# Low parts of four late weight matrices of layer 2, made in layer 1's MLP and read back from memory

## The chip, the cores and the metric

One core of one Trainium2 chip runs the whole program in one launch. The metric is the device time of one execution in microseconds; lower is better. PE is the matmul engine, DVE, ACT and POOL (GpSimd) are the vector, scalar and general engines, SP only issues transfers here.

## The reference

Two layers of a decoder trunk for 256 tokens of width 1024, all in float32. Of one layer (shortened):

```python
h = rms_norm(x, norm_mix[l]); z = h @ w_in[l]
...
o_all = jnp.stack([o_a, o_b, o_c], axis=2).reshape(B, T, N_MIXERS, MIX_WIDTH)
y = jnp.einsum('btnc,ncd->btnd', o_all, w_branch[l])
g = jax.nn.sigmoid(gm.reshape(B, T, N_MIXERS, D_MODEL))
x = x + jnp.sum(g * y, axis=2) @ w_out[l]
h2 = rms_norm(x, norm_mlp[l])
x = x + jnp.square(jax.nn.relu(h2 @ w_up[l])) @ w_down[l]
```

The mixers are A (sparse attention over the top keys of an indexer), B (sliding window with sinks) and C (compressed, selected and window branches).

## The kernel before

**Products in three parts.** Every weight is read once, as float32, and multiplied on PE in float32r. For float32 accuracy each 128 x 512 piece of a weight matrix is split (`wsplit`, L208): ACT copies it to float32r, the high part `wh` (L214), and DVE subtracts that from the raw piece, the low part `wl` (L215). `mm3` (L218) then makes three matmuls, activation high by `wh`, high by `wl`, low by `wh` (L219 to L221), for each of the two halves of 128 tokens, so six per piece. `raw` has 5 buffers of 128 x 1024 (two pieces), `wh` and `wl` 4 each.

```python
with tc.high_priority(offset=LEAD):
    wh = til(wsp, [P, 512], F32R, "wh")
    wl = til(wsp, [P, 512], F32R, "wl")
    act.copy(wh[:, :n], raw2d)
    dve.tensor_tensor(out=wl[:, :n], in0=raw2d, in1=wh[:, :n].bitcast(F32), op=ALU.subtract)
```

**The order of a layer.** `PLAN` lists the projections in the order in which `linear` (L223) streams them: queries, keys and values, the indexer, then the merge gates (gB1 is the gate of mixer B, columns 512 to 1023) and the branch projections (bB1 likewise). The last nine entries are gB1, gA1, gC1, bB1, bB0, bC0, gA0, bC1. Beside each piece a share of the attention of A, B or C is emitted, by the rate that stands next to the name; A's follows last. Then w_out and the MLP: `up` (L1041) makes 512 hidden columns from 8 pieces of w_up, `down` multiplies them by w_down, in the order up(0), up(1), down(0), up(2) and so on to up(7), down(6), down(7). In `up` each weight piece is the stationary side (L1052, L1053), and PE's results are squared and split by ACT and DVE (L1059 to L1065).

**What sets the order of instructions.** The code emits the work; a scheduler of the framework, with a simulated time line, then fixes the order on each engine, and the weight splits go 600 places ahead of where they are emitted (`LEAD`). At run time every engine works in that order and waits on semaphores. All loads of weights are issued by SP (L206, L243), in order. POOL has only a few multiplies for rotary (L356) and powers for the norms (L320, L465, L476).

**Between layer 1's w_out and its MLP** the new residual x (L1034) is transposed on PE, and each of the 16 blocks of 128 x 128 is scaled into `hT`: ACT makes its high part (L275), then DVE its low part (L276).

**Layer 2's late stage.** On the clock of the trace gA1 and gC1 run from about 606 to 630, bB1 and bB0 to about 649, then the attention of mixer C ends (L569 and L570 scores, L576 and L580 maximum, L587 exponential, L617 transposes, L200 and L201 their split, L646 a sum, L867 the compressed branch, L881 the selected branch), with pieces of bC0 between.

Of the kernel before, what the change touches and what calls it, by code (L numbers as in the profile page):

```python
# [8 lines left out]
F32 = mybir.dt.float32  # L9
F32R = mybir.dt.float32r  # L10
BF16 = mybir.dt.bfloat16
AF = mybir.ActivationFunctionType
ALU = mybir.AluOpType
# [3 lines left out]
P = 128  # L17
T = 256
NT = 2
D = 1024  # L20
# [3 lines left out]
DEPTH = 2  # L24
# [7 lines left out]
)  # L32
ACT_SET = "exp_and_others"
LEAD = 600
WARM = 9
SPLIT = 'A'
BUFS = dict(wraw=5, wsp=4, zp=3, mp=3, t4p=3, hlp=2, khp=2, pp=2, ptp=2, st=2, sm=3, gmp=3)

O_QA, O_KA, O_VA, O_IQ, O_IK, O_IW = 0, 512, 640, 768, 1024, 1088
O_QB, O_KB, O_VB = 1092, 1604, 1732  # L40
O_QC, O_KC, O_VC, O_KS, O_VS, O_KW, O_VW = 1860, 2372, 2500, 2628, 2756, 2884, 3012
O_GC, O_GM = 3140, 3164
# [50 lines left out]
def trunk(ctx: ExitStack, tc: tile.TileContext, A: dict, out: bass.AP):  # L93
    nc = tc.nc
    pe, dve, act, pool, sp = nc.tensor, nc.vector, nc.scalar, nc.gpsimd, nc.sync

    def mk(name, bufs=1, space=None):
        kw = {} if space is None else {"space": space}
        return ctx.enter_context(tc.tile_pool(name=name, bufs=bufs, **kw))
# [3 lines left out]
    wraw, wsp = mk("wraw", BUFS["wraw"]), mk("wsp", BUFS["wsp"])  # L103
    zp, mp, t4p = mk("zp", BUFS["zp"]), mk("mp", BUFS["mp"]), mk("t4p", BUFS["t4p"])
    hlp, khp = mk("hlp", BUFS["hlp"]), mk("khp", BUFS["khp"])
    qtp, vtp = mk("qtp", 2), mk("vtp")
    gmp, pp, ptp, otp = mk("gmp", BUFS["gmp"]), mk("pp", BUFS["pp"]), mk("ptp", BUFS["ptp"]), mk("otp", 2)
    fin = mk("fin", 2)
    st, sm = mk("st", BUFS["st"]), mk("sm", BUFS["sm"])
    ps_lin = mk("ps_lin", 4, PSUM)  # L110
    ps_s = mk("ps_s", 2, PSUM)
# [5 lines left out]
    def til(pool_, shape, dt, tag):  # L117
        uid[0] += 1
        return pool_.tile(shape, dt, tag=tag, name=f"{tag}_{uid[0]}")
# [13 lines left out]
    pieces = []  # L133
# [9 lines left out]
    with tc.high_priority(offset=0):  # L143
        act.dma_start(out=gcols, in_=A["gcols"])
        act.preload_act_table_set(ACT_SET)
        first_load(0, 1)
# [56 lines left out]
    def wload(src, kk, n):  # L203
        raw = til(wraw, [P, 1024], F32, "raw")
        v = raw[:, :kk * n].rearrange("p (k n) -> p k n", k=kk)
        sp.dma_start(out=v, in_=src)  # L206
        return v

    def wsplit(raw2d):
# [10 lines left out]
        pe.matmul(ps, lhsT=ah, rhs=bl, start=False, stop=False)  # L220
        pe.matmul(ps, lhsT=al, rhs=bh, start=False, stop=last)  # L221

    def linear(ps, xh, xl, w, c0, n, more=None):  # L223

        kc = w.shape[0] // P
        narrow = n <= 256
        kk, per = (4, 2) if narrow else (2, 1)
        c1, n1 = more or (0, 0)  # L230
        at_k = 0
        while at_k < kc:
            if pieces:
                raw = pieces.pop(0)
                kk = raw.shape[1]
            else:
                rows = slice(at_k * P, (at_k + kk) * P)
                raw = til(wraw, [P, 1024], F32, "raw")[:, :kk * (n + n1)].rearrange("p (k n) -> p k n", k=kk)
                early = ahead.pop() if ahead else 0
                for at, col, width in ((0, c0, n), (n, c1, n1)):  # L240
                    if width:
                        with tc.high_priority(offset=early):
                            sp.dma_start(out=raw[:, :, at:at + width], in_=w[rows, col:col + width].rearrange("(k p) n -> p k n", p=P))  # L243
            parts = []
            for j in range(0, kk, per):
                wh, wl = wsplit(raw[:, j:j + per, :].rearrange("p k n -> p (k n)"))
                for i in range(per):
                    cs = slice(i * (n + n1), (i + 1) * (n + n1))
                    parts.append((wh[:, cs], wl[:, cs]))
            steps = [(j, t) for j in range(kk) for t in range(NT)]  # L250
            if at_k + kk == kc:
                steps = [(j, t) for t in range(NT) for j in range(kk)]
            for j, t in steps:
                k, tk = at_k + j, slice(t * P, (t + 1) * P)
                mm3(ps[t][:, :n + n1], xh[:, k, tk], xl[:, k, tk], *parts[j], k == 0, k == kc - 1)
            at_k += kk
            yield kk * (n + n1) / 1024
# [33 lines left out]
    xh, xl = x_pair()  # L291
# [11 lines left out]
    for l in range(DEPTH):  # L303
        w_in = A["w_in"][l]
# [137 lines left out]
        def queries(m, c0, i):  # L442
            m.qT = til(qtp, [P, 8, T], F32R, "qT")
            m.rq = [til(lay, [P, 8], F32, f"rq{i}{t}") for t in range(NT)]
            ps = two_banks()
            yield from linear(ps, xh, xl, w_in, c0, 512)
            posts.append(queries_post(m, i, ps))

        def queries_post(m, i, ps):
# [254 lines left out]
        def branch_keys_1(m):  # L704
            m.kT = til(vtp, [P, 2, 2, 2, T], F32R, "kTC")
            m.v = [new_v(f"C{b}", F32R) for b in range(2)]
            ps = two_banks()
            yield from linear(ps, xh, xl, w_in, O_KC, 512)
            posts.append(branch_keys_1_post(m, ps))

        def branch_keys_1_post(m, ps):
# [183 lines left out]

        def gate_half(n, hf, dst, spare=None):
            ps = two_banks()
            yield from linear(ps, xh, xl, w_in, O_GM + n * D + hf * 512, 512)
            if n == 1:
                sg = pair[:, hf]  # L900
                dst[hf] = sg
            else:
                sg = til(vtp, [P, NT, 512], F32, spare) if spare else til(gmp, [P, NT, 512], F32, "sg")
                dst[hf] = sg
            for t in range(NT):
                act.activation(sg[:, t, :], ps[t], AF.Tanh, scale=hrstd[t])
# [3 lines left out]
        def branch_half(n, hf, m, sg):  # L910
            first = hf not in begun
            begun.add(hf)
            ps = two_banks()
            cs = slice(hf * 512, (hf + 1) * 512)
            yield from linear(ps, m.o[0], m.o[1], A["w_branch"][l][n], hf * 512, 512)
            for t in range(NT):
                y = merged[t][:, cs] if first else til(mp, [P, 512], F32, "m")
                dve.scalar_tensor_tensor(out=y, in0=sg[hf][:, t, :], scalar=1.0, in1=ps[t], op0=ALU.add, op1=ALU.mult)  # L918
                if not first:
                    dve.tensor_tensor(out=merged[t][:, cs], in0=merged[t][:, cs], in1=y, op=ALU.add)  # L920
# [35 lines left out]
        for hf in range(2):  # L956
            for key, n, m, sg in (("A", 0, MA, sgA), ("B", 1, MB, sgB), ("C", 2, C, sgC)):
                name = f"g{key}{hf}"
# [70 lines left out]
        for hf in range(2):  # L1029
            cs = slice(hf * 512, (hf + 1) * 512)  # L1030
            ps = two_banks()
# [8 lines left out]
        def up(gi):  # L1040
            L, S, X, O = (ps_lin, "lin"), (ps_s, "s"), (ps_t, "t"), (ps_o, "o")  # L1041
            ph = [bank(*b) for b in ((L, L, X, O) if gi == 0 else (S, S, L, L) if gi == 1 else (S, S, X, O))]
            src = A["w_up"][l][:, gi * 512:(gi + 1) * 512].rearrange("(a k p) n -> a p k n", p=P, k=2)
            for a in range(KC // 2):
                raw = wload(src[a], 2, 512)
                for j in range(2):
                    wh, wl = wsplit(raw[:, j, :])
                    k = 2 * a + j
                    for f in range(4):

                        fs = slice(f * P, (f + 1) * P)
                        pe.matmul(ph[f], lhsT=wh[:, fs], rhs=both_h[:, k].rearrange("p i t -> p (i t)"), start=k == 0, stop=False)  # L1052
                        pe.matmul(ph[f][:, :T], lhsT=wl[:, fs], rhs=hh[:, k, :], start=False, stop=k == KC - 1)  # L1053
            ah, al = new_o()
            for b in range(2):
                r = til(mp, [P, 512], F32, "m")
                for i in range(2):
                    part = r[:, i * T:(i + 1) * T]
                    act.copy(part, ph[2 * b + i][:, T:])  # L1059
                    dve.tensor_tensor(out=part, in0=ph[2 * b + i][:, :T], in1=part, op=ALU.add)  # L1060
                s = til(zp, [P, 512], F32, "z")
                dve.scalar_tensor_tensor(out=s, in0=r, scalar=0.0, in1=r, op0=ALU.max, op1=ALU.mult)
                s3 = s.rearrange("p (f q) -> p f q", f=2)
                act.copy(ah[:, 2 * b:2 * b + 2, :], s3)
                dve.tensor_tensor(out=al[:, 2 * b:2 * b + 2, :], in0=s3, in1=ah[:, 2 * b:2 * b + 2, :].bitcast(F32), op=ALU.subtract)  # L1065
            return ah, al

        def down(gi, a_):
# [9 lines left out]
            for f, hf in order:  # L1078
# [13 lines left out]
                elif f == 3:  # L1092
# [3 lines left out]
                                products(f_, hf, t)  # L1096
                    yield hf

        prev = up(0)
        for gi in range(1, NG):  # L1100
            nxt = up(gi)
            if gi == 1:
                acc = [[bank(ps_lin, "lin") for _ in range(NT)] for _ in range(2)]
            run(down(gi - 1, prev))
            prev = nxt
        r2 = []
        for t in range(NT):
            ss = sum_sq(t)
# [4 lines left out]
        if l + 1 < DEPTH:  # L1113
            xh, xl = x_pair()
# [39 lines left out]
```

## Time and profile before

| | us |
|---|---|
| median of 3 runs (916.27 to 917.17) | 916.95 |
| the profiled execution | 918.04 |
| its span | 916.3 |
| PE busy | 898.1 (98%) |
| DVE busy | 728.8 (80%) |
| ACT busy | 611.5 (67%) |
| POOL busy | 76.3 (8%) |
| layer 1's MLP, about | 281 to 467 |
| gA1, gC1, bB1, bB0 of layer 2, about | 606 to 649 |

A busy PE is only the sum of its instructions' stretches. What changes the time is where PE has nothing to do, so the table is a start and the stretches of PE's idle time are the thing to find: windows tell in which stage, the waits tell behind whom, and the timelines tell whether that engine was late or only its releaser.

### The profile page before, as it was taken

How to read it: one execution, taken by the hardware profiler on the slowest of the kernel's cores; microseconds unless marked ns; L12 is line 12 of the kernel's file. 1: busy time of each engine (PE TensorE's matmuls, PEld its weight loads, DVE VectorE, ACT ScalarE, POOL GpSimd, SP SyncE). 2: the span in 40 equal slices, each digit the busy share in tenths (PEclk: the TensorE clock that was granted, in tenths of full speed). 3: DMA queues.
4: the chain of work that ended last, by engine and by line, in shares of the span. 5: the costliest groups of instructions: out<-in, count | busy, mean ns of one | idle time of the engine just before them, and what ended most of it. 6: DMA issues, size and time to landing. Idle time of an engine off the chain costs nothing.

```text
span 916.3 us, 14300 instructions
## 1 busy us (share of the span) xinstructions
PE 898.1 (98%) x4785; PEld 749.6 (82%) x4785; DVE 728.8 (80%) x1558; ACT 611.5 (67%) x1369; POOL 76.3 (8%) x68
## 2 busy tenths in 40 slices
PE   8999999999999999999999999999899999999998
PEld 5888888877778888888879878878787788888886
DVE  5899989789986766666789999977998776666665
ACT  6787888767656655555578778877686575555553
POOL 0533011000000000000014420300000000000000
PEclk9999999999999999999999999999999999999999
DMA  8745556531455666666646555555134556666652
GB/s 301 211 141 168 161 162 184 161 115 60 128 174 167 199 192 193 194 185 188 193 137 187 165 157 170 177 181 151 61 93 137 182 162 208 185 187 196 191 184 92
DMA packets 84426, 153.15 MB, mean 167 GB/s; under 512 B 9600, under 2 KB 26880, under 8 KB 84352
## 3 DMA queue, kind: packets, MB, share of 16 engines
q1 hardware_dynamic: 84208, 152.22, 55.0%
q8 instruction: 37, 0.61, 0.3%
q14 instruction: 37, 0.30, 0.1%
q10 hardware_dynamic: 144, 0.02, 0.0%
HBM read 151.17 MB, written 1.05 MB: 166 GB/s over the span
## 4 chain that ended last, share of the span: by engine, by line
PE 84%; DVE 8%; issue 3%; DMA 2%; ACT 1%; POOL 1%; SPq 0%; DVEq 0%; ACTq 0%
PE lin L220 17%; PE lin L219 17%; PE lin L221 17%; PE s L1052 6%; PE s L1053 3%; DVE wl L215 3%; PE t L1052 3%; PE o L1052 3%; PE s L569 2%; DMA raw<-in_w_in 2%; PE lin L1052 2%; PE o L694 2%; PE t L1053 1%; PE o L1053 1%; PE t L617 1%
## 5 line engine op out<-in xcount | busy, mean ns | idle before, releaser
L215 DVE TENSOR_TENSOR wl<-raw,wh 128x512 fp32r<-128x512 f32 (+1 forms) x568 | 388.2, 693 | 139.2 <-ACT wh L214 134.6
L214 ACT CAST wh<-raw 128x512 fp32r<-128x512 f32 (+1 forms) x568 | 346.1, 619 | 209.2 <-PE lin L221 103.6
L220 PE MATMUL lin<-wl,xTh 128*128 128x512 f32 (+2 forms) x512 | 194.8, 384 | 3.7 <-DVE wl L215 3.2
L221 PE MATMUL lin<-wh,xTl 128*128 128x512 f32 (+2 forms) x512 | 187.0, 370 | 0.0
L219 PE MATMUL lin<-wh,xTh 128*128 128x512 f32 (+2 forms) x512 | 167.3, 379 | 1.6 <-ACT wh L214 1.6
L220 PE MATMUL lin<-wl,oTh 128*128 128x512 f32 x352 | 137.8, 392 | 0.0
L221 PE MATMUL lin<-wh,oTl 128*128 128x512 f32 x352 | 137.1, 391 | 0.0
L220 PEld LDWEIGHTS lin<-wl,xTh 128*128 128x128 f32 x512 | 96.2, 188 | 24.6 <-DVE wl L215 9.8
L219 PE MATMUL lin<-wh,oTh 128*128 128x512 f32 x352 | 113.5, 393 | 0.0
L219 PEld LDWEIGHTS lin<-wh,xTh 128*128 128x128 f32 x512 | 93.9, 189 | 19.0 <-ACT wh L214 3.6
L221 PEld LDWEIGHTS lin<-wh,xTl 128*128 128x128 f32 x512 | 96.0, 188 | 14.3 <-issue 0.2
L221 PEld LDWEIGHTS lin<-wh,oTl 128*128 128x128 f32 x352 | 66.1, 188 | 13.9 <-issue 0.2
L220 PEld LDWEIGHTS lin<-wl,oTh 128*128 128x128 f32 x352 | 66.1, 188 | 13.4 <-DVE hT L918 0.2
L1052 PE MATMUL s<-hT,wh 128*128 128x512 f32 x224 | 76.2, 395 | 0.0
L219 PEld LDWEIGHTS lin<-wh,oTh 128*128 128x128 f32 x352 | 65.2, 188 | 12.9
L587 ACT ACTIVATE pr<-s,mx,rq 128x256 f32<-128x256 f32 (+1 forms) x128 | 64.6, 517 | 1.3 <-DVE mx L580 1.3
L1053 PE MATMUL s<-hT,wl 128*128 128x256 f32 x224 | 52.7, 280 | 0.0
L1053 PEld LDWEIGHTS s<-hT,wl 128*128 128x128 f32 x224 | 42.1, 188 | 5.6
L1052 PE MATMUL t<-hT,wh 128*128 128x512 f32 x112 | 44.5, 397 | 0.0
L1052 PE MATMUL o<-hT,wh 128*128 128x512 f32 x112 | 44.0, 393 | 0.0
L1052 PEld LDWEIGHTS s<-hT,wh 128*128 128x128 f32 x224 | 38.6, 188 | 5.1
L200 ACT CAST pt<-t 128x512 fp32r<-128x512 f32 x36 | 21.2, 588 | 22.0 <-PE t L617 21.7
(202 smaller groups left out, 1328.8 us busy)
## 6 DMA issues: line engine op xcount, KB each, us to landing
raw<-in_w_in SPq DMA_DIRECT2D x91, 512.0 KB, 3.8
raw<-in_w_up SPq DMA_DIRECT2D x64, 512.0 KB, 3.8
raw<-in_w_down SPq DMA_DIRECT2D x64, 512.0 KB, 4.1
raw<-in_w_branch SPq DMA_DIRECT2D x24, 512.0 KB, 3.8
raw<-in_w_out SPq DMA_DIRECT2D x16, 512.0 KB, 3.8
raw<-in_w_ck SPq DMA_DIRECT2D x8, 512.0 KB, 3.9
raw<-in_w_cv SPq DMA_DIRECT2D x8, 512.0 KB, 4.2
raw<-in_w_in SPq DMA_DIRECT2D x8, 324.0 KB, 3.6
```

The costliest lines, as they stand in the source:

```text
L200: act.copy(hi, src)
L214: act.copy(wh[:, :n], raw2d)
L215: dve.tensor_tensor(out=wl[:, :n], in0=raw2d, in1=wh[:, :n].bitcast(F32), op=ALU.subtract)
L219: pe.matmul(ps, lhsT=ah, rhs=bh, start=first, stop=False)
L220: pe.matmul(ps, lhsT=ah, rhs=bl, start=False, stop=False)
L221: pe.matmul(ps, lhsT=al, rhs=bh, start=False, stop=last)
L569: pe.matmul(ps3[:, i * per:(i + 1) * per, :], lhsT=q[:, h, t * P:(t + 1) * P], rhs=rhs(j, h // 4), start=(i == 0 and j == 0), stop=False)
L587: act.activation(p3[:, r, :], ps3[:, r, :], AF.Exp, bias=mx[:, r:r + 1], scale=rq[r // per], accum_out=den[:, r:r + 1])
L617: pe.transpose(ps[:, i * P:(i + 1) * P], pr[:, i * P:(i + 1) * P], ident)
L694: pe.matmul(dst, lhsT=lhs_v(m.v, kt, g), rhs=p4[:, :, kt, :], start=i == 0 and kt == 0, stop=i == len(parts) - 1 and kt == t)
L1052: pe.matmul(ph[f], lhsT=wh[:, fs], rhs=both_h[:, k].rearrange("p i t -> p (i t)"), start=k == 0, stop=False)
L1053: pe.matmul(ph[f][:, :T], lhsT=wl[:, fs], rhs=hh[:, k, :], start=False, stop=k == KC - 1)
```

## The change

Four matrices of layer 2 are named in `STORED`: gA1, gC1 (8 pieces each), bB0, bB1 (4 each), 24 pieces. During layer 1's MLP a generator, `split_ahead`, makes one piece with each raw load of w_up from up(1) to up(6): SP loads the 256 KB piece (`pr`), ACT copies the high part (`pt`), DVE subtracts (`ptl`), SP stores the low part to memory. In layer 2, `linear` loads each raw piece of these matrices alone (256 KB in place of 512 KB for two), ACT makes `wh` as before, and a DMA that POOL issues brings the low part: odd pieces into the four `wl` buffers, even ones into two new buffers, `low`. `KEPT` is empty, so its branches don't run. All line numbers after the new code move: L215 is now L220, L219 to L221 are L224 to L226, L275 and L276 are L340 and L341, L867 and L881 are L932 and L946.

```diff
+KEPT = ()
+STORED = ('gA1', 'gC1', 'bB0', 'bB1')
...
+    lowp = mk("lowp", 2)
+    low_parts = mk("low_parts", 1, bass.MemoryType.DRAM)
...
-        sp.dma_start(out=v, in_=src)
+        last_load[:] = [sp.dma_start(out=v, in_=src).ins]
...
+    def split_ahead():
+
+        room = rooms()
+        for name in KEPT + STORED:
+            w, c0 = columns(1, name)
+            for k in range(w.shape[0] // P):
+                raw = til(pp, [P, 512], F32, "pr")
+                with tc.issue_after(last_load[0]):
+                    sp.dma_start(out=raw, in_=w[k * P:(k + 1) * P, c0:c0 + 512])
+                if name in KEPT:
+                    to = next(room)
+                    wh, wl = to[:, 0:512], to[:, 512:1024]
+                    kept.append((wh, wl))
+                else:
+                    wh, wl = til(ptp, [P, 512], F32R, "pt"), til(ptp, [P, 512], F32R, "ptl")
+                act.copy(wh, raw)
+                dve.tensor_tensor(out=wl, in0=raw, in1=wh.bitcast(F32), op=ALU.subtract)
+                if name in STORED:
+                    mem = til(low_parts, [P, 512], F32R, f"lo{name}{k}")
+                    sp.dma_start(out=mem.bitcast(F32), in_=wl.bitcast(F32))
+                    stored[name, k] = mem
+                yield
...
+            parts = []
+            if (name, at_k) in stored:
+                kk = 1
+                raw = til(wraw, [P, 1024], F32, "raw")
+                sp.dma_start(out=raw[:, 0:512], in_=w[at_k * P:(at_k + 1) * P, c0:c0 + 512])
+                wl = til(wsp, [P, 512], F32R, "wl") if at_k % 2 else til(lowp, [P, 512], F32R, "low")
+                pool.dma_start(out=wl, in_=stored[name, at_k])
+                with tc.high_priority(offset=LEAD):
+                    wh = til(wsp, [P, 512], F32R, "wh")
+                    act.copy(wh, raw[:, 0:512])
+                parts.append((wh, wl))
...
-            for j in range(0, kk, per):
+            for j in range(0, 0 if parts else kk, per):
...
                 raw = wload(src[a], 2, 512)
+                if gi:
+                    next(aside, None)
...
+        aside = split_ahead() if l + 1 < DEPTH else iter(())
...
+        for _ in aside:
+            pass
```

(`issue_after` places the load of `pr` behind the last raw load on SP.)

PE in the late stage, before, where the selected branch of mixer C begins (`lin_8025` is bC0, `o` the results of attention, `s` its scores, `t` its transposes):

```order
L219 MATMUL lin_8025<-wh_8029,oTh_7263 128x512
L220 MATMUL lin_8025<-wl_8030,oTh_7263 128x512
L221 MATMUL lin_8025<-wh_8029,oTl_7264 128x512
L219 MATMUL lin_8025<-wh_8033,oTh_7263 128x512
L220 MATMUL lin_8025<-wl_8034,oTh_7263 128x512
L221 MATMUL lin_8025<-wh_8033,oTl_7264 128x512
L867 MATMUL o_7507<-pt_7588,vcmp_5403 128x512
L569 MATMUL s_7692<-kTC_5522,qT_6118 128x256 x4
L570 LDWEIGHTS bcon
L570 MATMUL s_7692<-bcon 128x2x128
L617 MATMUL t_7603<-identr,pr_7559 128x128 x4
L881 MATMUL o_7598<-pt_7546,vSC_1315_5523 128x256 x2
```

and now (`lin_8195` and its wh_8236, wl_8234 are the end of bB0, `lin_8246` is bC0):

```order
L932 MATMUL o_7696<-pt_7779,vcmp_5600 128x512
L634 MATMUL s_7897<-kTC_5719,qT_6315 128x256 x4
L635 LDWEIGHTS bcon
L635 MATMUL s_7897<-bcon 128x2x128
L682 MATMUL t_7794<-identr,pr_7760 128x128 x4
L224 MATMUL lin_8246<-wh_8250,oTh_7460 128x512
L225 MATMUL lin_8246<-wl_8251,oTh_7460 128x512
L226 MATMUL lin_8246<-wh_8250,oTl_7461 128x512
L224 MATMUL lin_8246<-wh_8254,oTh_7460 128x512
L225 MATMUL lin_8246<-wl_8255,oTh_7460 128x512
L226 MATMUL lin_8246<-wh_8254,oTl_7461 128x512
L946 MATMUL o_7789<-pt_7747,vSC_1411_5720 128x256 x2
```

The six matmuls of bC0 stood ahead of `o` (L867) and the scores; they now stand behind the scores and the transposes, ahead of the first `o` of L881.

POOL before, at its end (`rq` are the last powers):

```order
L476 TENSOR_TENSOR rk_6505<-qss_6502,nhalf 128x4
L356 TENSOR_TENSOR m_7046<-z_7041,tabqs_5437 128x512
L356 TENSOR_TENSOR m_7066<-z_7043,tabqs_5437 128x512
L465 TENSOR_TENSOR rq_1640_6849<-qss_7087,nhalf 128x8
L465 TENSOR_TENSOR rq_1641_6850<-qss_7093,nhalf 128x8
```

and now (the names with logA, logC and lobB are the stored low parts of gA1, gC1 and bB):

```order
L530 TENSOR_TENSOR rq_1736_7046<-qss_7284,nhalf 128x8
L530 TENSOR_TENSOR rq_1737_7047<-qss_7290,nhalf 128x8
L291 DMA wl_7633<-logA_905_3770 128x512
L291 DMA wl_7728<-logA_923_3838 128x512
L291 DMA wl_7821<-logA_975_4022 128x512
L291 DMA wl_7874<-logA_993_4090 128x512
L291 DMA low_7769<-logA_966_3988 128x512
L291 DMA wl_7961<-logC_1041_4270 128x512
L291 DMA low_7862<-logA_984_4056 128x512
L291 DMA wl_8025<-logC_1059_4338 128x512
```

and so on to the 24th, two of which (`low` of logA_896 and logA_914) stand at the head of layer 2. The 22 of this place come behind POOL's last computation, in one row.

ACT at the beginning of layer 1's MLP, before (`t` are the sums of squares, `hT` the high parts of the normalised input):

```order
L275 ACTIVATE hT_3354<-s_3564,gcols 128x128
L275 ACTIVATE hT_3354<-s_3578,gcols 128x128
L275 ACTIVATE hT_3354<-s_3564,gcols 128x128
L214 CAST wh_3687<-raw_3673 128x512
L275 ACTIVATE hT_3354<-s_3578,gcols 128x128
L275 ACTIVATE hT_3354<-s_3564,gcols 128x128
L214 CAST wh_3725<-raw_3723 128x512
L275 ACTIVATE hT_3354<-s_3578,gcols 128x128
L275 ACTIVATE hT_3354<-s_3564,gcols 128x128
L214 CAST wh_3737<-raw_3723 128x512
L275 ACTIVATE hT_3354<-s_3578,gcols 128x128
L214 CAST wh_3751<-raw_3749 128x512
```

and now:

```order
L340 ACTIVATE hT_3359<-s_3569,gcols 128x128
L340 ACTIVATE hT_3359<-s_3583,gcols 128x128
L219 CAST wh_3692<-raw_3678 128x512
L267 CAST pt_3800<-pr_3798 128x512
L340 ACTIVATE hT_3359<-s_3569,gcols 128x128
L340 ACTIVATE hT_3359<-s_3583,gcols 128x128
L219 CAST wh_3738<-raw_3728 128x512
L340 ACTIVATE hT_3359<-s_3569,gcols 128x128
L340 ACTIVATE hT_3359<-s_3583,gcols 128x128
L267 CAST pt_3834<-pr_3832 128x512
L340 ACTIVATE hT_3359<-s_3569,gcols 128x128
L340 ACTIVATE hT_3359<-s_3583,gcols 128x128
```

Two copies for pieces to be stored (`pt`) now stand among the copies that make `hT`, where none stood. Two more `pt` stand before the first `hT`. On SP each load of `pr` follows the raw load that it belongs to, and the store of each `ptl` stands after one of the next loads, ahead of a later raw load.

## Rows read from the trace of the kernel before

**Rows 1.** The page, parts 1 and 2.

```profile
PE 898.1 (98%) x4785; PEld 749.6 (82%) x4785; DVE 728.8 (80%) x1558; ACT 611.5 (67%) x1369; POOL 76.3 (8%) x68
...
PEclk9999999999999999999999999999999999999999
```

**Rows 2.** Windows: stretch, its length; busy PE, PEld, DVE, ACT, POOL; clock, DMA share, GB/s.

```profile
606.00:630.00 24.00, 24.00 (x116) 19.66 (x116) 14.55 (x27) 16.46 (x42) 0.00 (x0) 1.00 0.54 175
630.00:649.00 19.00, 19.00 (x101) 15.65 (x100) 17.14 (x36) 12.49 (x30) 0.00 (x0) 1.00 0.52 149
649.00:664.00 15.00, 11.92 (x80) 9.77 (x79) 14.02 (x37) 9.32 (x26) 0.00 (x0) 1.00 0.06 24
...
312.00:445.00 133.00, 133.00 (x674) 112.98 (x673) 87.44 (x148) 73.56 (x133) 0.00 (x0) 1.00 0.63 191
```

**Rows 3.** All of PE's waits from 604 to 664.

```profile
PE o L881 <- DVE sum L646: 1.2, 1, 1.2
PE o L867 <- DVE pt L863: 1.1, 1, 1.1
PE s L569 <- ACT pr L587: 0.6, 1, 0.6
```

**Rows 4.** Lines of DVE from 606 to 649, the split's group.

```profile
L215 DVE TENSOR_TENSOR wl<-raw,wh 128x512 fp32r<-128x512 f32 x26 | 17.3, 688 | 8.8 <-ACT wh L214 8.8
```

**Rows 5.** Timeline of DVE: start, duration, instruction, [idle before, releaser].

```profile
649.59 0.69 DVE L576 TENSOR_REDUCE mx<-s 128x2 f32<-128x512 f32 x1 [0.17 <-PE s L570]
```

**Rows 6.** Timeline of PE, transposes of four blocks.

```profile
649.39 0.60 PE L617 MATMUL t<-identr,pr 128*128 128x128 f32 x4
```

**Rows 7.** Timeline of PE in gC1.

```profile
617.03 0.63 PE L219 MATMUL lin<-wh,xTh 128*128 128x512 f32 x2
...
618.44 0.40 PE L219 MATMUL lin<-wh,xTh 128*128 128x512 f32 x1
```

**Rows 8.** Timeline of POOL, 560 to 620.

```profile
579.25 1.73 POOL L356 TENSOR_TENSOR m<-z,tabqs 128x512 f32<-128x512 f32 x1 [34.05 <-DVE pr L602]
582.27 2.67 POOL L356 TENSOR_TENSOR m<-z,tabqs 128x512 f32<-128x512 f32 x1 [1.29 <-DVE m L366]
...
591.50 1.64 POOL L465 TENSOR_TENSOR rq<-qss,nhalf 128x8 f32<-128x8 f32 x1 [0.92 <-DVE qss L347]
```

**Rows 9.** DMA issues: KB of one, median us from issue to landing.

```profile
raw<-in_w_in SPq DMA_DIRECT2D x8, 324.0 KB, 3.6
...
out<-x SPq DMA_DIRECT2D x4, 256.0 KB, 2.0
raw<-in_w_in SPq DMA_DIRECT2D x2, 256.0 KB, 4.2
...
hT<-in_xT SPq DMA_DIRECT2D x1, 256.0 KB, 6.0
...
bcon<-in_bconsts SPq DMA_DIRECT2D x1, 240.0 KB, 8.7
```

**Rows 10.** Windows of the start-up.

```profile
5.00:10.00 5.00, 3.88 (x13) 2.23 (x12) 2.58 (x5) 1.92 (x5) 0.00 (x0) 1.00 0.93 311
10.00:15.00 5.00, 4.47 (x18) 3.14 (x18) 4.43 (x9) 4.78 (x10) 0.00 (x0) 1.00 1.04 393
```

**Rows 11.** Waits of PE's weight loads, 264 to 312.

```profile
PEld lin L1052 <- DVE hT L276: 0.6, 2, 0.3
```

**Rows 12.** Timeline of ACT at the start of the first MLP.

```profile
287.93 0.37 ACT L275 ACTIVATE hT<-s,gcols 128x128 fp32r<-128x128 f32 x1 [0.79 <-DVE hT L276]
...
289.84 0.62 ACT L214 CAST wh<-raw 128x512 fp32r<-128x512 f32 x1 [0.46 <-ACT hT L275]
```

**Rows 13.** Timelines of ACT, then PE, at the first hand-over.

```profile
307.19 0.65 ACT L214 CAST wh<-raw 128x512 fp32r<-128x512 f32 x1
...
308.17 0.84 PE L219 MATMUL lin<-wh,oTh 128*128 128x512 f32 x3
```

**Rows 14.** Lines from 312 to 445, the split's group.

```profile
L215 DVE TENSOR_TENSOR wl<-raw,wh 128x512 fp32r<-128x512 f32 x96 | 66.0, 689 | 45.4 <-ACT wh L214 44.7 <-PE s L1052 0.7
```

More of the change, by code (lines that the diff above doesn't have):

```diff
@@ L221, in mm3, with columns, rooms, linear @@
         pe.matmul(ps, lhsT=al, rhs=bh, start=False, stop=last)
-    def linear(ps, xh, xl, w, c0, n, more=None):
+    def columns(l, name):
+        if name[0] == "b":
+            return A["w_branch"][l]["ABC".index(name[1])], int(name[2]) * 512
+        at = {"qA": O_QA, "qB": O_QB, "qC": O_QC, "k1": O_KC}
+        for n in range(3):
+            for hf in range(2):
+                at[f"g{'ABC'[n]}{hf}"] = O_GM + n * D + hf * 512
+        return A["w_in"][l], at[name]
+    kept, stored = [], {}
+    last_load = []
+    def rooms():
+        for _ in range(BUFS["gmp"]):
+            yield til(gmp, [P, NT, 512], F32, "sg").rearrange("p t n -> p (t n)").bitcast(F32R)
+        for _ in range(2):
+            q = til(qtp, [P, 8, T], F32R, "qT").rearrange("p h t -> p (h t)")
+            yield q[:, 0:1024]
+            yield q[:, 1024:2048]
+        yield til(hlp, [P, 8, P], F32R, "qhl").rearrange("p h q -> p (h q)")
+    def split_ahead():
[19 more added lines that the diff above has]
+                yield
+    def linear(ps, xh, xl, w, c0, n, more=None, name=None):
         kc = w.shape[0] // P
@@ L232, in linear @@
         while at_k < kc:
-            if pieces:
+            parts = []
[9 more added lines that the diff above has]
+                parts.append((wh, wl))
+            elif kept:
+                kk = 2
+                parts += [kept.pop(0), kept.pop(0)]
+            elif pieces:
                 raw = pieces.pop(0)
@@ L243, in linear @@
                             sp.dma_start(out=raw[:, :, at:at + width], in_=w[rows, col:col + width].rearrange("(k p) n -> p k n", p=P))
-            parts = []
-            for j in range(0, kk, per):
+            for j in range(0, 0 if parts else kk, per):
                 wh, wl = wsplit(raw[:, j:j + per, :].rearrange("p k n -> p (k n)"))
@@ L445, in queries @@
             ps = two_banks()
-            yield from linear(ps, xh, xl, w_in, c0, 512)
+            yield from linear(ps, xh, xl, w_in, c0, 512, name=l and f"q{'BAC'[(1, 0, 2).index(i)]}")
             posts.append(queries_post(m, i, ps))
@@ L707, in branch_keys_1 @@
             ps = two_banks()
-            yield from linear(ps, xh, xl, w_in, O_KC, 512)
+            yield from linear(ps, xh, xl, w_in, O_KC, 512, name=l and "k1")
             posts.append(branch_keys_1_post(m, ps))
@@ L897, in gate_half @@
             ps = two_banks()
-            yield from linear(ps, xh, xl, w_in, O_GM + n * D + hf * 512, 512)
+            yield from linear(ps, xh, xl, w_in, O_GM + n * D + hf * 512, 512, name=l and f"g{'ABC'[n]}{hf}")
             if n == 1:
@@ L914, in branch_half @@
             cs = slice(hf * 512, (hf + 1) * 512)
-            yield from linear(ps, m.o[0], m.o[1], A["w_branch"][l][n], hf * 512, 512)
+            yield from linear(ps, m.o[0], m.o[1], A["w_branch"][l][n], hf * 512, 512, name=l and f"b{'ABC'[n]}{hf}")
             for t in range(NT):
```

## Prediction

> **What bounds the kernel now.** I read the page first: PE is busy for 98% of the span and its granted clock stands in the top tenth in all 40 slices [rows 1]. So only two things can move the time: idle time of PE that goes, or idle time that comes. The number of matmuls doesn't change. The profiled execution took 918.04 us, span 916.3, which is 1.09 above the median 916.95 of the runs; I make the sum as a difference and put it on the median. About 0.2% (1.83 us) is what a measurement of this kernel can tell from no change.
>
> Next I read the windows [rows 2]. From 606 to 649 (gA1, gC1, bB1, bB0: the four matrices whose low parts are no longer subtracted) PE has no idle time, though DVE is busy 17.14 of 19.00 us in the second half. From 649 to 664 PE works 11.92 of 15.00: 3.08 us idle. There DVE works 14.02 of 15.00 and DMA is nearly idle, so DVE is the bound. The chain of PE's waits names the three places: 1.2, 1.1 and 0.6 us, all behind DVE or ACT work of attention, none behind a low part [rows 3]. From 312 to 445, most of the MLP that takes the new work, PE is never idle and DVE has 45 us free, ACT 59.
>
> **What goes.** 24 of 26 subtractions of 0.69 us leave DVE between 606 and 649, 16.6 us in all [rows 4]. PE wasn't idle there, so this is worth nothing where it stands. Could DVE enter the tail earlier? Its max at 649.59 starts after 0.17 us of waiting for the scores of PE: DVE had just caught up [rows 5]. From there to 664 the list of DVE's work is as before, so its pace stays, and with it most of PE's idle time.
>
> **What moves.** On PE the six bC0 matmuls that stood before L867's `o` now stand behind the transposes, ahead of the first selected-block `o`, which was the one that waited 1.2 us [rows 3]. Six matmuls take 618.44 − 617.03 = 1.41 us [rows 7]. They no longer delay the scores, and they fill that wait: **−1.4 us**. The other two waits have the same DVE work ahead of them as before, and stay. The most it could be is the whole idle time of the stage, −3.1; the least is 0, if DVE follows PE later by as much.
>
> **What is added in layer 2: 24 loads of low parts on POOL's queue.** POOL's last compute ends at 593.1 [rows 8], before these loads, and nothing is queued behind them but one another. The odd ones go into the four `wl` buffers and are asked for 6 us of PE work or more ahead, by counting matmuls in the order. The even ones have two buffers of their own: a load can start only when PE has read the `low` two before, and must land before PE reads its own. By the order, between the last read of low_7621 and the first of low_7769 (gA1, k = 4) stand 15 matmuls of 512 columns and three small ones: 15 × 1.41 / 6 = 3.5 [rows 7], and about 0.1 each for the small ones (four transposes in 0.60, the end of the last included [rows 6]): 3.8 us. The next ones have 5.7 (gA1, k = 6), 5.4 and 5.05 (gC1, k = 0 and 2), then 6.3 and more.
>
> No 256 KB load by POOL is in the trace. What is the time L from issue to landing? The nearest rows: SP's 324 KB takes 3.6, a pair of 256 KB 4.2; in the crowd of the start 256 KB took 6.0 and 240 KB 8.7 [rows 9]. The demand of these stages comes near that crowd: 256 KB more per 2 × 1.41 us of raw and low together, twice the 149 to 175 GB/s of before, 300 to 350, against 311 and 393 at the start [rows 2, 10]. At L = 3.6 nothing is late. At 4.2 the first is late by 0.4, at 5.0 by 1.2. At 6.0 four are late, by 2.2, 0.3, 0.6 and 0.95, some 3.2 together as a stall of one lengthens the next one's distance; at 8.7 all ten are, some 17. I take L = 5.0, between the quiet 3.6 to 4.2 and the crowded 6.0, nearer to the quiet ones since the raw loads are now single 256 KB pieces: **+1.2** (ends 0 and +17).
>
> The Trainium skill, page "DMA: Bandwidth & Descriptors", section on the anatomy of a DMA of GpSimd's path, fits such a transfer as 2.0 us plus its bytes over 436 GB/s: an estimate of 2.6 us for 256 KB. By that no low part would be late and the sum would be 1.2 lower, 917.4; no row of this trace shows a transfer of this size as quick except the stores of the output, 2.0.
>
> **What is added in the first layer's MLP: 24 loads, 24 ACT copies (0.62 [rows 12]), 24 DVE subtractions (0.69), 24 stores, 12.6 MB.** In the steady part that is at most 24 × 0.69 = 16.6 us on DVE and 24 × 0.62 = 14.9 on ACT, where 45 and 59 are free, and 12.6 MB in some 133 us take DMA from 191 to about 286 GB/s, under the 311 of the start: **0**. SP has the stores in line with the raw loads, each waiting for a `ptl`; five `raw` buffers stand before it. If that cover were gone, each raw load would be as late as the `pr` before it.
>
> At the start of that MLP there is no slack. The normalised input is made by a relay of ACT (`hT`, L275) and DVE (L276), and PE's first matmuls wait for it twice, 0.6 us together [rows 11]. In the order two of the first four `pt` copies stand inside that relay on ACT, and their `ptl` on DVE; two stand just before. One pair costs 0.62 + 0.69 = 1.31 if nothing hides it. ACT has 0.79 and 0.46 us of idle time there, part of it because it waits for DVE [rows 12]. I take one pair: **+1.3** (ends 0 and 4 × 1.31 = 5.2). A second place is the next hand-over: `wh` of 307.19 ends 0.33 us before its matmuls at 308.17, behind four copies of `m` [rows 13], and now a `pt` of 0.62 stands among those copies: **+0.6** (ends 0 and 1.3).
>
> **Sum:** −1.4 + 1.2 + 0 + 1.3 + 0.6 = +1.7, so 916.95 + 1.7 = 918.6.
>
> **Rivals.**
> - *Covered everywhere* (the other side). A POOL load lands in less than 3.8 us and the relay takes the `pt` copies into ACT's idle time. For it: the quiet row of 3.6, ACT's gaps. Against: the demand, and a relay that PE already waits for. What is left is the gain of 1.4 to 3.1: 915.6 to 913.9. It decides at L = 3.8 and at less than 0.6 us of unhidden work in the relay.
> - *Low parts late throughout.* L is 6 to 7, for want of DMA share or because GpSimd is held up while DVE works: the same POOL multiply of L356 took 1.73 and then 2.67 us [rows 8]. That replaces 1.2 by 3.2 to 7.6 (at 7, seven are late): +3.7 to +8.1, 920.6 to 925.0. It decides from L of about 5.5. [...]
> - *MLP bound by the new loads.* A `pr` that lands late stops ACT and DVE, and the `wl` behind it. The steady part has 96 `wl` in 133 us [rows 14], one per 1.39; the closest `ptl` stands four of them behind its load, 5.5 us. With the 0.62 of ACT, a landing after 4.9 us is late, and by the crowd's 6.0 to 8.7 it is so by 1.1 to 3.8. One stop of 2 us in each of six groups gives +12, 929. Against: the four buffers of `wl` let DVE run ahead, and 34% of it is free.
> - *Nothing moves.* PE's order shift wins nothing, and all costs are hidden: 916.9. For it: PE was idle for none of the removed work.
>
> **How the numbers follow.** Forecast 0.45 (own range 916.5 to 920.6; about half of it under 0.2%), covered everywhere 0.22 (a third of that still within 0.2%), low parts late 0.20, MLP bound 0.03, nothing moves 0.10. Faster: 0.15 + 0.01 = 0.16. Same: 0.23 + 0.07 + 0.10 = 0.40. Slower: 0.21 + 0.20 + 0.03 = 0.44. The range goes from the upper part of the covered case, 915.2, to the middle of the late case, 923.5.
>
> **What would show it.** In the changed profile: PE's idle stretch before the first selected-block `o` is gone, the other two stay; PE waits about 1 us for a `low` at gA1's k = 4; PE waits for `hT` near 289 to 292 more than before; the DMA table gives the POOL loads about 5 us. Wrong it is if PE is idle in 312 to 445, or if DVE's tail ends much earlier than 664 against its start.

## The result, and the profile after

The change took 926.47 us (median of 4 runs, 924.56 to 931.02) where the kernel before took 916.88 beside it: ratio 1.0106, 95% interval 1.009 to 1.0122. Measured once more in a later series it took 926.64 against 917.54, 1.0102 (1.0085 to 1.012). The forecast was 918.6, with a range up to 923.5. It is slower, as the largest of the three chances (0.44) had it, but by more than five times the forecast's 1.7 us, and outside the range.

The profiled execution of the change took 924.56 us, the fastest of the four, with a span of 922.6, 6.3 more than before. The page's first lines answer to [rows 1]:

```profile
PE 899.9 (98%) x4785; PEld 748.7 (81%) x4785; DVE 725.9 (79%) x1558; ACT 619.9 (67%) x1393; POOL 90.2 (10%) x92
...
PEclk9999999999999999999999999999999999999999
```

PE has the same number of matmuls and the same clock. By the page 4.5 of the 6.3 us are idle time of PE and 1.8 are busy time, but most of the second belongs to waits too: matmuls follow one another every 1.41 / 6 = 0.235 us [rows 7], while the record of one lasts about 0.39, so about 0.16 us of each wait of PE doesn't show as idle (an estimate from these rows). The windows say where the idle time is. The first MLP, before and after (281 to 313 holds its start and first hand-over, 313 to 440 the steady part; columns as in [rows 2]). The kernel before:

```profile
281.00:313.00 32.00, 31.98 (x174) 27.17 (x173) 25.65 (x52) 21.64 (x47) 0.00 (x0) 1.00 0.58 173
313.00:440.00 127.00, 127.00 (x648) 108.02 (x647) 81.62 (x137) 69.79 (x127) 0.00 (x0) 1.00 0.64 193
```

The change:

```profile
281.00:313.00 32.00, 27.89 (x153) 23.24 (x152) 23.92 (x51) 21.32 (x47) 1.31 (x2) 1.00 0.77 256
313.00:440.00 127.00, 125.71 (x632) 105.75 (x632) 91.61 (x154) 74.82 (x141) 0.00 (x0) 1.00 0.81 264
```

PE was idle for 0.02 us in these 159 us, and is now for 4.11 + 1.29 = 5.4. In the second profile of the change it is 4.78 + 3.28 = 8.1 us, with a span of 924.7:

```profile
281.00:313.00 32.00, 27.22 (x150) 22.69 (x149) 23.15 (x50) 21.11 (x46) 1.31 (x2) 1.00 0.78 253
313.00:440.00 127.00, 123.72 (x618) 103.40 (x617) 90.67 (x153) 74.00 (x141) 0.00 (x0) 1.00 0.80 259
```

The starts of the same matmuls count the hidden part as well. A line gives the shortest, middle and longest of its matmuls in ns, then the first and the last start: `lin<-hT,wh` begins up(0), `lin<-wh,oTl` stands in `down` alone. The kernel before:

```profile
L1052 PE MATMUL lin<-hT,wh x32: 389/395/498, 281.6 to 305.2; 128*128 128x512 f32 x32
L221 PE MATMUL lin<-wh,oTl x128: 389/389/398, 306.1 to 460.7; 128*128 128x512 f32 x128
```

The change:

```profile
L1119 PE MATMUL lin<-hT,wh x32: 389/395/503, 280.9 to 307.7; 128*128 128x512 f32 x32
L226 PE MATMUL lin<-wh,oTl x128: 387/389/398, 308.6 to 467.0; 128*128 128x512 f32 x128
```

From the first start to the last the MLP took 460.7 − 281.6 = 179.1 us and now takes 186.1, 7.0 more; in the second profile of the change it is 10.2 more. (In the kernel before it ends at about 461, not at 467.) So nearly all of the loss lies in the first layer's MLP, and its size differs from one profile to the next. Behind whom PE waits there, in the change (us in total, times, longest):

```profile
PE lin L224 <- ACT wh L219: 2.4, 2, 1.2
PE lin L1119 <- DVE hT L341: 1.7, 2, 1.2
PE lin L1119 <- ACT wh L219: 1.2, 1, 1.2
```

Before, the same view has no row for 270 to 470. Both releasers are ACT or come from ACT, yet ACT is busy for only 74.82 of 127 us. The lines of ACT from 275 to 470, the `pt` group, tell what it does instead (busy and mean, then idle time ahead of it and what ended that):

```profile
L267 ACT CAST pt<-pr 128x512 fp32r<-128x512 f32 x24 | 14.9, 620 | 28.4 <-DMA pr<-in_w_in 18.3 <-DMA pr<-in_w_branch 10.0
```

ACT **stands still at the new copies for 28.4 us, until their loads have landed**. ACT works in order, so the casts of w_up and w_down behind a `pt` and the high parts of `hT` stand with it. The timeline of ACT at the start of the MLP shows it:

```profile
289.03 0.62 ACT L267 CAST pt<-pr 128x512 fp32r<-128x512 f32 x1 [0.74 <-DMA pr<-in_w_in]
...
294.18 0.62 ACT L267 CAST pt<-pr 128x512 fp32r<-128x512 f32 x1 [2.67 <-DMA pr<-in_w_in]
294.71 0.62 ACT L340 ACTIVATE hT<-s,gcols 128x128 fp32r<-128x128 f32 x2
295.22 1.13 ACT L219 CAST wh<-raw 128x512 fp32r<-128x512 f32 x2
```

and PE's own timeline, the wait that comes of the second one:

```profile
295.89 0.73 PE L1119 MATMUL lin<-hT,wh 128*128 128x512 f32 x2 [1.16 <-ACT wh L219]
```

The loads aren't unusually slow: DMA issues, KB and median us to landing, with those of layer 2:

```profile
pr<-in_w_in SPq DMA_DIRECT2D x16, 256.0 KB, 4.3
...
pr<-in_w_branch SPq DMA_DIRECT2D x8, 256.0 KB, 4.8
...
low<-logA POOLq DMA_DIRECT2D x4, 256.0 KB, 4.1
wl<-logA POOLq DMA_DIRECT2D x4, 256.0 KB, 3.8
wl<-logC POOLq DMA_DIRECT2D x4, 256.0 KB, 5.1
low<-logC POOLq DMA_DIRECT2D x4, 256.0 KB, 4.8
wl<-lobB POOLq DMA_DIRECT2D x4, 256.0 KB, 5.7
low<-lobB POOLq DMA_DIRECT2D x4, 256.0 KB, 4.3
```

The 24 loads of `pr` land in 3.6 to 6.1 us, 4.5 in the median. The copies stand too near behind them in ACT's order: the load of 288.01, the slowest, was read by a copy that ACT reached at 291.5, 3.5 us after its issue. The same subtraction for all 24 copies gives 1.9 to 5.5 us, 3.5 in the median. A second path isn't seen: SP stood for 27.4 us at stores that waited for a `ptl`, ahead of later raw loads, but no copy or subtraction of a `raw` piece waited for a load in this MLP.

Layer 2's late stage, in the change (windows of 6 us later than those of before):

```profile
612.00:636.00 24.00, 23.73 (x118) 19.36 (x118) 5.19 (x13) 16.38 (x43) 7.56 (x14) 1.00 1.02 322
636.00:655.00 19.00, 19.00 (x99) 15.40 (x98) 12.91 (x30) 13.21 (x30) 2.16 (x4) 1.00 0.83 257
655.00:670.00 15.00, 13.01 (x81) 10.04 (x79) 13.56 (x36) 8.67 (x26) 0.00 (x0) 1.00 0.17 54
```

and all of PE's waits there, against [rows 3]:

```profile
PE o L932 <- DVE pt L928: 0.9, 1, 0.9
PE s L634 <- ACT pr L652: 0.6, 1, 0.6
PE lin L225 <- DMA low<-logC: 0.3, 1, 0.3
PE o L946 <- DVE ptl L206: 0.2, 1, 0.2
```

The wait before the first selected-branch `o` is gone, the two others stayed. The stage's idle time fell from 3.08 to 1.99 us, and one low part came 0.3 us late. DVE is much freer (5.19 of 24 us in place of 14.55), and that buys nothing, as PE wasn't waiting for it.

### The profile page after: what moved, and what is told of

The parts are those of the page before. It is cut to its first block, busy times and chain, and to the rows that moved or that the text cites. A ratio compares the mean times of both kernels' runs of the same rounds, so it can differ in the third digit from the quotient of the medians.

```text
span 922.6 us, 14501 instructions
## 1 busy us (share of the span) xinstructions
PE 899.9 (98%) x4785; PEld 748.7 (81%) x4785; DVE 725.9 (79%) x1558; ACT 619.9 (67%) x1393; POOL 90.2 (10%) x92
## 4 chain that ended last, share of the span: by engine, by line
PE 75%; DVE 11%; DMA 5%; issue 4%; ACT 3%; POOL 1%; SPq 0%; DVEq 0%; POOLq 0%; ACTq 0%
PE lin L225 16%; PE lin L226 15%; PE lin L224 15%; PE s L1119 5%; DVE wl L220 4%; PE s L1120 3%; PE t L1119 3%; PE o L1119 3%; PE s L634 2%; DMA raw<-in_w_in 2%; PE t L682 1%; PE o L759 1%; PE t L1120 1%; PE lin L1119 1%; PE o L1120 1%
## 5 line engine op out<-in xcount | busy, mean ns | idle before, releaser
L220 DVE TENSOR_TENSOR wl<-raw,wh 128x512 fp32r<-128x512 f32 (+1 forms) x544 | 370.5, 694 | 108.1 <-ACT wh L219 103.6
L219 ACT CAST wh<-raw 128x512 fp32r<-128x512 f32 (+1 forms) x544 | 329.0, 618 | 172.5 <-PE lin L226 80.1
L225 PE MATMUL lin<-wl,xTh 128*128 128x512 f32 (+2 forms) x496 | 188.3, 383 | 3.7 <-DVE wl L220 3.2
L226 PE MATMUL lin<-wh,xTl 128*128 128x512 f32 (+2 forms) x512 | 187.2, 370 | 0.0
L224 PE MATMUL lin<-wh,xTh 128*128 128x512 f32 (+2 forms) x512 | 168.1, 378 | 1.4 <-ACT wh L219 1.4
L226 PE MATMUL lin<-wh,oTl 128*128 128x512 f32 x352 | 137.9, 393 | 0.0
L225 PE MATMUL lin<-wl,oTh 128*128 128x512 f32 x344 | 134.3, 391 | 0.0
L224 PE MATMUL lin<-wh,oTh 128*128 128x512 f32 x352 | 114.0, 394 | 2.5 <-ACT wh L219 2.4
L225 PEld LDWEIGHTS lin<-wl,xTh 128*128 128x128 f32 x496 | 93.1, 188 | 23.7 <-DVE wl L220 9.7
L224 PEld LDWEIGHTS lin<-wh,xTh 128*128 128x128 f32 x512 | 93.7, 188 | 18.6 <-ACT wh L219 3.1
L226 PEld LDWEIGHTS lin<-wh,xTl 128*128 128x128 f32 x512 | 96.0, 188 | 14.2 <-issue 0.2
L224 PEld LDWEIGHTS lin<-wh,oTh 128*128 128x128 f32 x352 | 64.8, 188 | 16.8 <-ACT wh L219 3.9
L226 PEld LDWEIGHTS lin<-wh,oTl 128*128 128x128 f32 x352 | 66.1, 188 | 13.9 <-issue 0.2
L206 DVE TENSOR_TENSOR ptl<-t,pt 128x512 fp32r<-128x512 f32 x36 | 24.7, 687 | 17.9 <-ACT pt L205 17.5
```

The source lines that it names most:

```text
L206: dve.tensor_tensor(out=lo, in0=src, in1=hi.bitcast(F32), op=ALU.subtract)
L224: pe.matmul(ps, lhsT=ah, rhs=bh, start=first, stop=False)
```

## The experiments

All ratios are to the kernel before, run on the same chip beside them.

**1. early3: load the pieces three steps ahead of their copies.** The loads stay at their places in the program, and each copy is emitted three steps later. Six pieces' room comes from the gate buffers `sg`, idle in the MLP.

```diff
-                raw = til(pp, [P, 512], F32, "pr")
+            while len(raws) < min(i + 1 + 3, len(jobs)):
...
+                if len(raws) % 2 == 0:
+                    room = til(gmp, [P, NT, 512], F32, "sg")
+                raw = room[:, len(raws) % 2, :]
...
+            act.copy(wh, raws[i])
```

> Each piece to be split is loaded three steps earlier, into buffers that stand idle in the MLP; the order of PE and ACT is that of the change. Theory 1 (ACT stands at a pt until its load has landed, 28.4 us in all in the change, and what is behind it on ACT comes late): ACT's waits at pt fall below 5 us, PE's idle time in the first layer's MLP from 5.4 us to under 1.5, time 916 to 919. Theory 2 (the 24 copies and subtractions themselves are too much for the relay): 924 to 927, as the change. Theory 3 (281 GB/s are too much for the loads of w_up and w_down): 923 to 927, as the traffic is the same.

Measured: 927.12, ratio 1.0106 (1.0092 to 1.0119), as the change. Theory 1 missed its number. But the wait was still there: in this kernel's lines of ACT the copies wait as long as in the change.

```profile
L270 ACT CAST pt<-sg 128x512 fp32r<-128x512 f32 x24 | 14.9, 620 | 27.9 <-DMA sg<-in_w_in 17.3 <-DMA sg<-in_w_branch 10.6
```

The order of the instructions says why: although the program emits a copy three steps behind its load, the scheduler put every one of them back. In the two traces ACT's 1393 instructions stand in the same order, one by one. That it goes by the landing which its own time line gives the load is likely, but not shown. So the edit didn't do what it was for, and the run tells nothing of the theories.

**2. no_load: no loads; the copies read the w_up piece just loaded.**

```diff
-                raw = til(pp, [P, 512], F32, "pr")
-                with tc.issue_after(last_load[0]):
-                    sp.dma_start(out=raw, in_=w[k * P:(k + 1) * P, c0:c0 + 512])
+                raw = last_raw[0]
```

> Leaves out the 24 loads of the pieces: the copies and subtractions work on the piece of w_up that has just been loaded, so the stored low parts are of other data; copies, subtractions, stores and the loads by GpSimd stay. Theory 1: 916 to 919. Theory 2: 924 to 927. Theory 3: 918 to 921, as half of the added traffic is gone.

Measured: 924.57, ratio 1.0094 (1.0076 to 1.0112). Again the number of theory 1 was missed, and again the wait was not removed but only changed its transfer:

```profile
L267 ACT CAST pt<-raw 128x512 fp32r<-128x512 f32 x24 | 15.0, 625 | 27.7 <-DMA raw<-in_w_up 27.7
```

It does speak against theory 3: with 6.3 MB less traffic (228 GB/s in 313 to 440, where the change has 264) the loss is nearly the same. A part of it is PE's clock. PE stood for 3.61 us at once in the relay, and from 293 to 295 its granted clock was 0.51, about the lower of its two levels (1.2 of 2.4 GHz). PE's timeline, then the window:

```profile
292.04 0.80 PE L1119 MATMUL lin<-hT,wh 128*128 128x512 f32 x1 [3.61 <-DVE hT L341]
293.00:295.00 2.00, 2.00 (x8) 1.71 (x7) 1.21 (x4) 1.34 (x4) 0.50 (x1) 0.51 0.82 200
```

A pair of matmuls took 0.64 us there and 0.35 after 295, so from 292.0 to 294.8 some 1.2 us went this way (an estimate from these starts).

**3. mlp_only: the first MLP's side alone.**

```diff
-            if (name, at_k) in stored:
+            if False:
```

> Makes and stores the low parts in the first layer's MLP as the change does, but layer 2 splits its weights as before and doesn't read them. Theories 1 to 3 alike: the loss is all here, 924 to 929. Rival (low parts that come late in layer 2 cost several us): 919 to 922, with the rest in layer 2.

Measured: 924.94, ratio 1.0089 (1.0075 to 1.0103). Nearly all of the loss is in the MLP.

**4. layer2_only and layer2_free: layer 2's side alone.** The first makes one low part and stores it, and all 24 loads of GpSimd read that one; the second stores a piece of x in its place and splits nothing. The edit of the first:

```diff
-                    stored[name, k] = mem
-                yield
+                    for n_ in STORED:
+                        for k_ in range(columns(1, n_)[0].shape[0] // P):
+                            stored[n_, k_] = mem
+                yield
+                return
```

> One low part is made and stored in the first layer's MLP, and all 24 loads of GpSimd in layer 2 read that one, so 23 of the low parts are of other data. It prices layer 2's side alone. Theories 1 to 3: 916 to 918, gain and loss of the late stage cancel. Rival (late low parts): 919 to 922. If the filled wait of PE is worth what was forecast and no low part is late: 914.5 to 916.

> Layer 2's side alone, with nothing split in the first layer's MLP: one 256 KB piece of x is stored there, and all 24 loads of GpSimd read it in place of the low parts. layer2_only gave +1.8 us with one pt copy that still waited 2.3 us for its load at the start of the MLP. Theory 1: without that wait 915.5 to 918, gain and loss of the late stage cancel. If late low parts cost what layer2_only lost: 918 to 920.

Measured: layer2_only 919.09, ratio 1.002 (1.0005 to 1.0035); layer2_free 917.72, ratio 1.0002 (0.9991 to 1.0013). The one `pt` copy of layer2_only was enough to cost something: ACT waited 2.3 us for its load, and PE then 1.3 for `hT`, its only wait in that MLP. Without the copy, in layer2_free, PE doesn't wait there at all. The late stage wins and loses nothing that can be measured, though layer2_free had PE waiting 0.8 us for `low` parts.

**5. late_copy: early3, and each copy tied behind the newest cast ahead of it in the program.** `last_cast` is the instruction of the last `wh` copy in `wsplit`; the edit is against early3's kernel.

```diff
-            act.copy(wh, raws[i])
+            with tc.issue_after(last_cast[0]):
+                act.copy(wh, raws[i])
```

> As early3, but each pt copy is also tied on ACT behind the newest cast of w_up that precedes it in the program, so that it stands three steps behind its load; in early3 the scheduler had put the copies back to where they were. Traffic, copies, subtractions and stores are those of the change. Theory 1 (ACT stands at a load): ACT's waits at pt under 3 us (28 in the change), PE never idle in the first layer's MLP, 916 to 919. Theory 2 (the instructions themselves) and theory 3 (the traffic): 923 to 927 with no wait at a pt.

Measured: 917.55, ratio 0.9999 (0.9991 to 1.0007). All of the loss is gone. In this kernel's lines of ACT, no copy waits at all:

```profile
L272 ACT CAST pt<-sg 128x512 fp32r<-128x512 f32 x24 | 14.8, 616 | 0.0
```

and in its windows PE has 0.03 us of idle time:

```profile
281.00:313.00 32.00, 31.97 (x174) 27.19 (x173) 26.33 (x54) 22.99 (x49) 0.77 (x1) 1.00 0.74 238
313.00:440.00 127.00, 127.00 (x649) 108.17 (x648) 95.04 (x161) 80.97 (x150) 0.54 (x1) 1.00 0.85 278
```

The same copies, subtractions, loads and stores are there, and the traffic of the steady part is higher than in the change (278 GB/s). Its loads even land later, 5.1 us in the median. So theory 1 stands and theory 3 falls. Theory 2 falls for the copies of the steady part; those at the start late_copy also moves out of the relay, so what their work alone costs there is left to x_copy.

**6. x_copy: the work without any load.** The copies read x, which lies in SBUF, tied as in late_copy.

```diff
-                raw = til(pp, [P, 512], F32, "pr")
-                with tc.issue_after(last_load[0]):
-                    sp.dma_start(out=raw, in_=w[k * P:(k + 1) * P, c0:c0 + 512])
+                raw = xs[0][:, 0:512]
...
-                act.copy(wh, raw)
+                with tc.issue_after(last_cast[0]):
+                    act.copy(wh, raw)
```

> Leaves out the 24 loads: the copies and subtractions read the residual x, which lies in SBUF, so the stored low parts are of other data; the copies are tied behind the casts as in late_copy, without the three steps. One of them still stands inside the relay that makes hT. Theory 1: 916 to 919, nothing waits for a transfer. Theory 2: 923 to 927. Theory 3: 917 to 920.

Measured: 918.36, ratio 1.0012 (1.0002 to 1.0022). This kernel has one copy inside the relay, and its PE waits once in that MLP:

```profile
287.85 0.97 PE L1119 MATMUL lin<-hT,wh 128*128 128x512 f32 x3 [0.64 <-ACT wh L219]
```

That is what one copy in the relay cost by its work alone: 0.64 us. The change has two there, so of its 9.6 us some 1.3 could be work and not waiting (an estimate from this one wait).

**7. start_free and start_tied: late_copy with the first four copies free, or only these tied.**

```diff
-            with tc.issue_after(last_cast[0]):
-                act.copy(wh, raws[i])
+            if i >= 4:
+                with tc.issue_after(last_cast[0]):
+                    act.copy(wh, raws[i])
+            else:
+                act.copy(wh, raws[i])
```

(start_tied has `i < 4`.)

> As late_copy, but the first four pt copies, those at the start of the MLP, are not tied and stand where the change has them, two of them inside the relay. The traces of the change and of early3 put 3 to 5 us of PE's loss before 312 us and 2 to 4 after it. Theory 1: ACT's waits at pt are those of the first four alone, 5 us, and the time 919.5 to 923.

> The other half: the first four copies are tied as in late_copy, the twenty of the later groups are not. Theory 1: 919 to 923, with start_free's loss about the 9 us of the change in sum. If the loss were the relay alone (the step of the prediction, only larger): 916.5 to 918.

> The change itself, once more, beside the two kernels that follow: 924 to 928. Theory 1: ACT's waits at pt again near 28 us.

Measured: the change again 926.64, with ACT standing for 31.3 us at the copies; start_free 921.49, ratio 1.0039 (1.0026 to 1.0053); start_tied 921.78, 1.0042 (1.0029 to 1.0055); the change 1.0102. By these times each half costs about 4 us, together 0.81% of the change's 1.02%, whose interval goes down to 0.85%. Not all of it is in the MLP: the profiled executions of both have a span 4.2 us longer than the kernel before, of which the starts of the matmuls put 2.7 (start_free) and 2.2 (start_tied) into that MLP. Most of the rest of start_tied is in layer 2's late stage: PE waited 1.0 us for a `low` of gA1, and its granted clock was 0.50 from 664 to 666. That the other executions of the two lose their 4 us in the same places isn't shown.

The MLP's length by these starts, in us, as a difference to the kernel before (24.5 and 154.6), up to the first `lin<-wh,oTl` (up(0) and up(1), with the relay) and from there to the last one:

| | up to `down` | from there |
|---|---|---|
| the change, first and second profile | +3.2, +3.6 | +3.8, +6.6 |
| mlp_only | +2.0 | +5.7 |
| start_free | +3.1 | −0.4 |
| start_tied | 0.0 | +2.2 |
| x_copy | +0.7 | −0.2 |
| late_copy | 0.0 | −0.3 |

In start_free ACT waits 5.0 us, all at the first copies; in start_tied 18.7 us for loads, at the twenty others. So a microsecond of standing costs most where the relay has no slack, but the later groups, where I had put 0, cost 2.2 us in start_tied, and in the change the part that holds them cost more than the relay. Why start_tied has less of it than the change wasn't looked into.

No version came out ahead of the kernel before; the best, late_copy, equals it.

## Why the prediction was wrong, point by point

- **What bounds the kernel** and **what goes**: right. Taking 16.6 us of subtractions from DVE won nothing where they stood.
- **What moves** (−1.4): right in kind. The wait of 1.2 us went, and the idle time of the stage's last 15 us fell by 3.08 − 1.99 = 1.1.
- **Low parts late** (+1.2, by L = 5.0 and a wait at gA1's k = 4): oversized for the change. The POOL loads took 3.8 to 5.7 us by their groups' medians, and `low` for gA1 4.1; PE waited 0.3 us, in gC1. In the other profiles that read these parts it waited between 0 (late_copy) and 1.0 us (start_tied, at gA1's k = 4, as forecast). The Trainium skill, page "DMA: Bandwidth & Descriptors", section on the anatomy of a DMA, gives an estimate of 2.6 us for such a transfer; in these stages, at 257 to 322 GB/s, the measured times are longer, and they decide. The sum of the late stage was forecast at −0.2 us; layer2_free has it at +0.2 (−0.8 to +1.2). That the sums agree owes something to luck, as both terms came out smaller in the change.
- **The steady part of the MLP, "0"**: this is the step that failed. I compared the work, 14.9 us on ACT, with the free time, 59, and where I looked for a wait, in the rival, I counted from the `ptl` on DVE: 5.5 us behind its load, 4.9 for the copy. ACT reached the copies 3.5 us behind their loads in the median, and the loads landed after 4.5, so ACT stood at 22 of the 24. `pt` stands on ACT, in order, ahead of the casts that PE needs next, and ACT's free time was no cover, for it lay behind the copy, not ahead of it. Together with the next hand-over this part was forecast at +0.6 us; it took 3.8 and 6.6 more in the change's two profiles. start_tied, where the copies of the start don't wait, still has 2.2 of it.
- **The start of the MLP, "+1.3" and "+0.6"**: right place, too small a price. I priced one copy and subtraction by their durations. By work alone a copy there costs 0.64 us (x_copy). What it costs beside that is the rest of its load's flight, up to 2.67 us of ACT's time at one copy: up to the first `lin<-wh,oTl` the change took 3.2 and 3.6 us more, and start_free, where these four copies alone wait, 3.1. At the hand-over PE's wait for `wh` is 1.2 us. Also, the 0.6 us of [rows 11] that I took for waits of PE's matmuls are waits of its weight loads, which overlap its matmuls: PE itself was idle for 0.02 us from 281 to 313.
- **The rival "MLP bound by the new loads"** had the mechanism, a stop of ACT at a late `pr` and of the `wl` behind it. I gave it 0.03, with free time on DVE as the reason against. late_copy shows that without this wait nothing of the loss is left; up to 1.3 us of it may be the work of the two copies in the relay. That the rival's +12 is near the measured +9.6 is luck: it took one stop of 2 us in each of six groups, and there were 22 stops of 1.3 us in the mean. **"Nothing moves"** is the time that late_copy has.
- The range was too narrow for the same reason: the ends of the MLP's steady term, 0, were not bounded by a landing time as those of layer 2's loads were. (Its upper end isn't the middle of the late case either: 920.6 to 925.0 has 922.8. That decides nothing here.)

## What to carry to other kernels

Work that is put into another engine's idle time brings its waits along. Price it on each in-order engine by where its operand's load will land, not by its duration against the engine's free share: the instruction must stand far enough behind its load that it never waits, or the needed work behind it waits too. Where a scheduler with a time line of its own sets the order, look for the place that it gave the copy, and tie the copy to an instruction that comes late enough, as late_copy does beside its lead of three steps; emitting it later in the program alone changed nothing here.

And before moving work off an engine ask whether anything waited for it: here PE was never idle in the 43 us, 606 to 649, in which DVE was relieved of 16.6 us of subtractions.

## What the runs showed of the hardware

Loads of the same 256 KB took 3.6 to 6.1 us in the change's MLP. By the median of the loads from w_in they took 4.3 and 4.5 us in the change's two profiles, where DMA moved 264 and 259 GB/s, 4.7 in early3 at 260 and 5.1 in late_copy at 278. In layer 2, at 322 and then 257 GB/s, GpSimd's loads by group medians were between 3.8 and 5.7 us, SP's raw pieces of the same size 4.4 and 5.2. The Trainium skill, page "SBUF — State Buffer", warns in the section on SBUF's two separate sides that GpSimd can't write the descriptors of its transfers while DVE runs an operation in a two-port mode, and says in the section on who interferes with whom that `tensor_tensor`, the subtractions here, has no such mode; no run here shows GpSimd's loads slower than SP's.

In two of the profiles PE's granted clock shows a stretch at about half: in no_load after PE had stood for 3.61 us (0.51 from 293 to 295), and in start_tied after shorter waits of 0.6 and 0.9 us in the late stage (0.50 from 664 to 666). The change has these shorter waits too, at a clock of 1.00.

The change spread over 924.56 to 931.02 us in its first series and 926.23 to 929.55 in the second, the kernel before over 916.27 to 917.17 and, in its longest series, 914.23 to 919.70. Whether the scatter of landings adds to the scatter of the time isn't shown.
